# Half-array matmuls of a state mixing and of two attentions, reordered to alternate between the array's halves

## The chip, the cores and the metric

The kernel runs on one core of a Trainium2 chip, as one launch. The metric is the device time of a launch in microseconds; three runs of the kernel before took 2068.22, 2066.45 and 2060.09 us, median 2066.45. The core's engines work side by side, each through its own queue of instructions in order: PE (matmuls, with its weight loads shown apart as PEld), DVE (vector), ACT (activations), POOL (elementwise work off PSUM) and SP (which issues DMAs here). PE writes its results to PSUM, which has eight banks of 128 partitions by 512 fp32 values. PE's array has 128 rows (the contracted index, read from SBUF partitions) and 128 columns (the output's partitions). A matmul that needs only part of them names its corner with `tile_position=(row, column)`.

## The reference

Two layers over 512 latent tokens and 256 context tokens, 1024 features wide. Each layer: norm and modulation, an input projection, two mixers side by side, an output projection, and an MLP with squared ReLU. The parts that matter here:

- layer 0, attention: each of 8 query heads of 64 features (4 to each of 2 key heads) attends to all keys; latent queries see 6 tiles of 128 keys, context queries the 2 tiles of the context. Softmax, then the weighted sum of the values.
- layer 0, state mixing, in both directions over the tokens, per head with a 64x64 state S:

```
sa = S kk_t
S  = S * w_t - sa (kk_t * a_t) + v_t k_t
y_t = S r_t
```

- layer 1, attention: latent queries see the context, their own tile and its neighbours within 128 tokens, and a sink logit.
- layer 1, a second state model (chunks of 128 tokens), which the change touches by one buffer only.

## The kernel before, in words

Everything is written against a planner. The Python code emits instructions in an order that gives each a priority (`tc.high_priority()` raises it). The planner then fixes each engine's order before the run, from priorities and from when inputs are ready on its simulated timeline, and puts in the waits. Tiles with a tag share a number of buffers (`bufs`).

The first layer's mixers run in one phase (lines 846 to 1172). The state mixing goes by chunks of 32 tokens, 24 steps, each of which does one chunk of each direction `d`, with four pairs of heads `a`. The two heads `h` of a pair lie on the halves of the partitions, and the results of the two directions on the halves of the output's partitions. In `step` (lines 972 to 1021) a chunk goes: x from the state (line 987), `xs` on DVE, u (line 997, 32x32 corners), the two `vu` on DVE, the state's update s (line 1012), and the new state on DVE, which the next step's x needs. `prepare` (lines 908 to 970) makes, ahead of it, the products z (line 946) and xv (line 963). `outputs` (lines 1023 to 1042) makes y from the state (line 1032) and from `vu` (line 1033). x, xv and y are matmuls of 128 rows by 64 columns, with 64 moving columns, on column half `64 * d`. s uses 64 rows and 64 columns, in the corner (64 h, 64 h).

Before, x and xv ran through all four `a` of one direction and then of the other. y did so too, with the state's and the `vu` product of each `a` in turn. s ran through all directions and pairs of head 0 and then of head 1.

`attend` (lines 1088 to 1134) is the attention, a generator whose steps fill in between (`advance(fill)`); 40 of its steps come ahead of the state mixing. For each query tile and each half `g` of the heads it makes four heads' scores and their softmax into `prob` tiles. Then for each key tile four transposes go into a `pt` bank (line 1124), a copy of it goes to `pts` by DVE or ACT in turn (lines 1127 and 1129), and a value matmul goes into `po` (line 1130): 128 rows of keys, 64 columns, 512 moving columns. Half `g` of the heads took column half `g` of the array, accumulated over the key tiles, so that all matmuls of one `g` stood on one column half. `po` has one PSUM bank and `pt` two. A copy of `po` (line 1133) goes out by DMA at the end of the query tile.

`attend1` (lines 1476 to 1524) is the same for layer 1's four latent query tiles, with 4 or 5 key tiles each, one `pt` bank, and line 1518 for the value matmul. Its result is split at once into high and low parts in the place of the queries. `go` advances it at high priority, beside the input projection's column tiles, then beside the second state model (`own`, `rest`, `states`) and the first half of the output projection.

Of the kernel before, what the change touches and what calls it, by code (L numbers as in the profile page):

```python
# [18 lines left out]
P = 128  # L19
# [16 lines left out]
# the latents in the order in which the mixers finish them: the tiles in the middle, then the two outer ones  # L36
# [3 lines left out]
# order of the 128-token tiles and of the 64-token blocks for each direction  # L40
# [3 lines left out]
# column tiles of the second layer's input projection  # L44
F1_ORDER = ["B0", "B1", "C0", "C1", "x0", "x1", "x2", "x3", "k", "v", "q0", "q1", "q2", "q3"]
CONV_INDEX = {n: i for i, n in enumerate(["x0", "x1", "x2", "x3", "B0", "B1", "C0", "C1"])}
# column tiles of the first layer's input projection, in the order of their use
# [5 lines left out]
class Cols:  # L53
    """Named column ranges of a packed [128, n] array."""
# [15 lines left out]
def feat(a):  # L70
    """[..., n*128] -> [128, ... * n] with feature p of tile t in row p."""
    a = np.asarray(a)
    a = a.reshape(a.shape[:-1] + (a.shape[-1] // P, P))
    return np.moveaxis(a, -1, 0).reshape(P, -1)
# [41 lines left out]
def masks():  # L116
    """Constants of the second layer only."""
    f = np.float32
    c = Cols()
    m, n = np.arange(P)[:, None], np.arange(P)[None, :]  # L120
    c.add("upto", (m <= n).astype(f))
    c.add("from", (m >= n).astype(f))
    c.add("neg0", np.where(m > n, f(-1e30), f(0)))
    c.add("neg1", np.where(m < n, f(-1e30), f(0)))
    return c
# [38 lines left out]
# rows of the state mixing's output: tiles (a // 2, head of the pair), in them (a % 2, feature)  # L164
# [3 lines left out]
def tiles_k(w):  # L168
    """[K, n*128] -> [n, 128, K/128 * 128]: per column tile, the K tiles side by side."""
# [4 lines left out]
def pack(i):  # L174
# [8 lines left out]
    # the first layer's modulation weights: [group of 2048 columns, k tile, half, 128, 1024]  # L183
    o["wmod"] = np.ascontiguousarray(i["w_mod"].reshape(2, KT, P, 3, 2, 1024).transpose(0, 3, 1, 4, 2, 5)[0].reshape(3, KT, 2, P, 1024)[1:])
    # the second layer's: a column tile's columns in the rows, (row of the K tile, K tile) along them
    o["wmod1"] = np.ascontiguousarray(i["w_mod"][1].reshape(KT, P, 48, P).transpose(2, 3, 1, 0).reshape(48, P, D))
    # the first group's by quarters of the features: [quarter, pair of k tiles, 128, (k tile, shift or scale, 256)]
# [11 lines left out]
    # z: tokens by features, per half of the features two pieces of four K tiles  # L199
# [5 lines left out]
    # [layer, group, pair of column tiles, 128, (column tile, k tile, 128)]  # L205
# [5 lines left out]
class Stream:  # L211
    """The residual of both streams, tile by tile."""
# [12 lines left out]
def tile_trunk(ctx: ExitStack, tc: tile.TileContext, t: dict, out, cc: Cols, pc: Cols):  # L225
# [20 lines left out]
    # the unit matrix and the ones first  # L246
# [14 lines left out]
    def psum_pool(stack, side="left", **tags):  # L261
        """PSUM of a phase: per tag, its number of tiles and of banks per tile, or the tag that it shares."""
# [3 lines left out]
    def psum(tag, name):  # L266
# [3 lines left out]
        if isinstance(v, list):  # L270
            # in turn
# [5 lines left out]
    def split(hi, lo, src, lo_eng=None):  # L277
        """hi + lo = src exactly, each in the 12 bits that one pass carries."""
# [12 lines left out]
    def cols2(seg):  # L291
        """Columns of a two-bank PSUM tile that hold a segment's tokens."""
        return slice(256 + seg[0], 256 + seg[0] + seg[1])

    def at(t, s):
        """A segment's columns of t, [128, tokens]."""
# [4 lines left out]
    def like(t, s):  # L301
        """Side by side columns in the shape of a segment's."""
        return t.rearrange("p (b c) -> p b c", c=P) if s == OUTER else t

    class Split:
        """A PSUM tile [128, tokens] whose streams lie in a bank each."""
# [7 lines left out]
    class One(Split):  # L314
        """A PSUM tile that holds a segment."""
# [4 lines left out]
        def __call__(self, s):  # L320
            return self.ps[:, 0:s[1]]

# [9 lines left out]
    def product(items, xh, xl, ks, segs, first=True, last=True, k0=0):  # L332
        """ps[128, tokens] (+)= W^T x for the K tiles ks and each of the items (ps, W, first column in W), K tile by K tile.

        W and x as hi and lo parts; W's K tiles count from k0 on."""
# [10 lines left out]
    # ---------------------------------------------------------------- modulation  # L346
    def sigmoid(out, in_, tmp, halfbias=None):
        """1 / (1 + exp(-x)) = (tanh(x / 2) + 1) / 2."""
# [6 lines left out]
    def rsqrt(out, in_, scale, eps, n):  # L355
        """(in_ * scale + eps) ** -0.5 of n columns."""
# [15 lines left out]
    def modulation(l, j):  # L372
        """Shift, scale and gate columns 2048 j.. of layer l, one K tile per step."""
# [21 lines left out]
    def first_modulation(q, np_):  # L395
        """Shift and scale of the first layer's projections, for a quarter of the features."""
# [27 lines left out]
    def norm_scale(l, which, wname, a=None, k=0, n=KT):  # L424
        """norm weight * (1 + scale), per feature and stream."""
# [10 lines left out]
    # ---------------------------------------------------------------- norms  # L436
# [3 lines left out]
    def add_squares(np_, acc, x, k, s, eng=G):  # L440
        """Adds the squares of feature tile k to the sums of a stream's tokens."""
# [7 lines left out]
    def rms_rows(np_, acc, s, tag):  # L449
        """1 / rms of each of a stream's tokens, broadcast over the partitions."""  # L450
# [18 lines left out]
    def norm_tile(np_, x, bc, a, l, shift, hh, hl, s, k, eng):  # L469
        """hi and lo parts of x / rms * a + shift, feature tile k."""  # L470
# [10 lines left out]
    def norm_mod(np_, x, acc, a, l, shift, hh, hl, s, tag):  # L481
        """hi and lo parts of x / rms * a + shift."""
# [5 lines left out]
    # ---------------------------------------------------------------- layer 0: projections and what needs no state  # L488
# [16 lines left out]
    with ExitStack() as sa:  # L505
# [4 lines left out]
        # 1 - mu_prev - mu_next  # L510
# [3 lines left out]
        with ExitStack() as sx:  # L514
# [13 lines left out]
            # the first column tiles go along with the quarters of the features  # L528
# [23 lines left out]
        # sums start again with every chunk  # L552
# [18 lines left out]
        def shifted(n, name, bufs=2, ps=None, copy=False):  # L571
            """Column tile n, mixed with the tokens before and after within its stream."""
# [15 lines left out]
        def tile_of(ps, i):  # L588
            """Columns of the i-th 128 tokens."""
# [3 lines left out]
        def token_sums(ps, c, sq):  # L593
            """Per token and half of the partitions, the sum of sq: columns c.. of ps."""
# [3 lines left out]
        def token_broadcast(r, name):  # L598
            """[tokens, (tile, half)] -> a row per token, over the partitions of each half."""
# [32 lines left out]
        def load_k(p):  # L632
            """Keys of a pair of heads, and their unit vectors."""
# [17 lines left out]
        def load_v(p):  # L651
            v = vs[p] = shifted(5 + 3 * p, "fv", 2)
            # tokens of v to the partitions
# [1138 lines left out]
```

## Time and profile before

| | |
|---|---|
| median of 3 runs | 2066.45 us |
| lowest, highest | 2060.09, 2068.22 us |
| span of the profiled execution | 2059.2 us |
| its mean granted TensorE clock | 0.977 |
| state mixing and attention, first x to last po | 397.7 to 703.3 us |
| layer 1's value matmuls, first to last | 1448.0 to 1658.3 us |

The profile is of one execution, and its span runs from the first to the last instruction; the launch's own time was not recorded apart from the three runs, which lie 0.9 to 9.0 us above that span. In the rows, "L987" is line 987 of the kernel, `x<-state,ard` names the tile written and those read, and `128*64 128x64` is rows by columns of the array and the moving operand. Each fp32 matmul leaves two records, each with its weight load. A matmul's duration includes its latency through the array, so that neighbours overlap in the records.

### The profile page before, as it was taken

To read this page: it belongs to the slowest core of one execution; us is meant where nothing else is said; L and a number is where in the kernel's file an instruction comes from. 1 tells how busy PE (TensorE), PEld (TensorE's weight loads), DVE (VectorE), ACT (ScalarE), POOL (GpSimd) and SP (SyncE) were. 2 spreads that over 40 slices of the span, in tenths; PEclk is the share of its full clock that TensorE was granted. 3 is DMA by queue.
4 is the path that set the end of the run, shared out by engine and by line. 5 is a ranking of instruction groups with operands and counts; after the bars stand their busy time and mean duration, and the time that the engine had idled before them with its cause. 6 is when DMAs were issued, how large, how long until landed. Compare 5 with 4: busy or idle time off the path is not lost.

```text
span 2059.2 us, 34221 instructions
## 1 busy us (share of the span) xinstructions
PE 1945.9 (94%) x13992; PEld 1593.0 (77%) x13992; DVE 1211.2 (59%) x2057; ACT 826.5 (40%) x1397; POOL 374.2 (18%) x379
## 2 busy tenths in 40 slices
PE   6999978799999989999999999999979999999997
PEld 4776656587777689888888888888856888888886
DVE  6466889556456666565455443677577574444445
ACT  4333333344444354222222332545466654333335
POOL 0033268322122152000000000321033120000002
PEclk9999998699999999999999999999999999999998
DMA  8445455742231473333444442311100133333333
GB/s 318 136 146 195 164 189 149 156 91 49 65 76 35 130 237 110 103 123 119 134 127 124 128 128 72 104 56 56 58 21 1 52 123 91 94 92 102 93 94 112
DMA packets 148173, 229.24 MB, mean 111 GB/s; under 512 B 65056, under 2 KB 102320, under 8 KB 147888
## 3 DMA queue, kind: packets, MB, share of 16 engines
q1 hardware_dynamic: 141200, 214.59, 34.7%
q10 hardware_dynamic: 5456, 7.73, 1.2%
q0 software_dynamic: 1360, 4.73, 0.7%
q8 instruction: 110, 1.80, 0.4%
q14 instruction: 47, 0.39, 0.1%
HBM read 200.53 MB, written 26.48 MB: 110 GB/s over the span
## 4 chain that ended last, share of the span: by engine, by line
PE 74%; DVE 11%; DMA 6%; POOL 3%; issue 3%; ACT 3%; SPq 0%; DVEq 0%; POOLq 0%; ACTq 0%
PE m L343 36%; PE win L343 10%; DMA wmod<-in_wmod_dram 4%; PE po L1130 2%; PE z L946 2%; PE s L1012 2%; DVE wlo L280 2%; PE po L1518 2%; PE pt L1124 2%; PE sc L1109 1%; PE y L1033 1%; PE wout L1276 1%; DVE junk L1293 1%; PE z L1548 1%; PE y L1032 1%
## 5 line engine op out<-in xcount | busy, mean ns | idle before, releaser
L279 ACT ACTIVATE whi<-wraw 128x1024 fp32r<-128x1024 f32 x214 | 226.4, 1059 | 663.8 <-PE m L343 561.5
L280 DVE TENSOR_TENSOR wlo<-wraw,whi 128x1024 fp32r<-128x1024 f32 x214 | 264.8, 1239 | 196.3 <-ACT whi L279 193.7
L343 PE MATMUL m<-hh,whi 128*128 128x512 f32 (+1 forms) x816 | 240.4, 344 | 3.8 <-ACT relu L1215 2.2
L343 PE MATMUL m<-hh,wlo 128*128 128x512 f32 (+1 forms) x816 | 241.5, 344 | 0.4 <-DVE wlo L280 0.4
L343 PE MATMUL m<-hl,whi 128*128 128x512 f32 (+1 forms) x816 | 241.5, 343 | 0.2 <-POOL hl L479 0.2
L343 PE MATMUL m<-dl,whi 128*128 128x256 f32 (+1 forms) x832 | 240.7, 341 | 0.0
L343 PE MATMUL m<-dh,whi 128*128 128x256 f32 (+1 forms) x832 | 238.6, 342 | 2.1 <-DVE xl L1197 1.9
L343 PE MATMUL m<-dh,wlo 128*128 128x256 f32 (+1 forms) x832 | 239.8, 341 | 0.1
L447 POOL TENSOR_TENSOR acc<-acc,nsq 128x256 f32<-128x256 f32 x42 | 43.2, 1036 | 854.0 <-ACT nsq L446 853.3
L343 PEld LDWEIGHTS m<-dh,whi 128*128 128x128 f32 x832 | 153.3, 188 | 24.2 <-DVE xl L1197 5.3
L343 PEld LDWEIGHTS m<-hh,whi 128*128 128x128 f32 x816 | 152.6, 188 | 23.7 <-ACT relu L1215 2.6
L343 PEld LDWEIGHTS m<-hh,wlo 128*128 128x128 f32 x816 | 153.4, 188 | 19.8 <-DVE wlo L280 1.1
L343 PEld LDWEIGHTS m<-hl,whi 128*128 128x128 f32 x816 | 153.6, 188 | 19.3 <-POOL hl L479 0.4
L343 PEld LDWEIGHTS m<-dl,whi 128*128 128x128 f32 x832 | 153.8, 188 | 19.0
L343 PEld LDWEIGHTS m<-dh,wlo 128*128 128x128 f32 x832 | 153.6, 188 | 18.9 <-DVE wlo L280 0.3
L343 PE MATMUL win<-hl,whi 128*128 128x512 f32 (+1 forms) x512 | 161.7, 349 | 4.9 <-POOL hl L479 3.5
L343 PE MATMUL win<-hh,whi 128*128 128x512 f32 (+1 forms) x512 | 158.2, 355 | 1.7 <-ACT hh L474 1.6
L343 PE MATMUL win<-hh,wlo 128*128 128x512 f32 (+1 forms) x512 | 159.0, 344 | 0.0
L1293 DVE SCALAR_TENSOR_TENSOR junk<-wmod,crow 128x1024 f32<-128x1024 f32 x64 | 78.4, 1225 | 115.4 <-DMA wmod<-in_wmod_dram 114.9
L1197 DVE SCALAR_TENSOR_TENSOR xl<-m,modT,xl 128x512 f32<-128x512 f32 (+1 forms) x144 | 97.3, 685 | 72.3 <-PE m L343 72.3
L343 PEld LDWEIGHTS win<-hh,whi 128*128 128x128 f32 x512 | 95.5, 193 | 29.1 <-issue 7.2
L343 PEld LDWEIGHTS win<-hl,whi 128*128 128x128 f32 x512 | 98.2, 193 | 20.8 <-POOL hl L479 4.7
(411 smaller groups left out, 3717.0 us busy)
## 6 DMA issues: line engine op xcount, KB each, us to landing
wraw<-in_w_dram SPq DMA_DIRECT2D x136, 512.0 KB, 3.5
wmod<-in_wmod_dram SPq DMA_DIRECT2D x96, 512.0 KB, 4.2
wraw<-in_wout_dram SPq DMA_DIRECT2D x40, 512.0 KB, 3.6
wraw<-in_win_dram SPq DMA_DIRECT2D x35, 512.0 KB, 3.9
arD<-ar SPq DMA_DIRECT2D x8, 768.0 KB, 3.8
kbD<-kb SPq DMA_DIRECT2D x8, 768.0 KB, 4.4
ari<-arD SPq DMA_DIRECT2D x24, 256.0 KB, 3.8
kbd<-kbD SPq DMA_DIRECT2D x48, 128.0 KB, 3.7
```

Source lines behind the costliest of these rows:

```text
L279: A.activation(out=hi, in_=src, func=AF.Copy)
L280: (lo_eng or V).tensor_tensor(out=lo, in0=src, in1=hi.bitcast(F32), op=ALU.subtract)
L343: T.matmul(part(ps, s), lhsT=a[:, c], rhs=row(b, k, s), start=first and j == 0 and q == 0, stop=last and j == n - 1 and q == 2)
L447: (V if k == KT - 1 else eng).tensor_tensor(out=at(acc, s), in0=at(acc, s), in1=at(sq, s), op=ALU.add)
L946: T.matmul(ps[:, P * (2 * a + c):P * (2 * a + c) + P], lhsT=kb[:, 2 * m + a, c, :], rhs=ar[:, 2 * m + a, c, :], start=True, stop=True)
L1012: T.matmul(pd[r, 256 * d + 64 * a:256 * d + 64 * a + 64], lhsT=zs[d][r, a, cl[d], 64:128], rhs=vu[d][r, a, :], start=True, stop=True, tile ...
L1032: T.matmul(o, lhsT=ars[d][:, a, c, 0, :], rhs=state[:, d, a, :], start=True, stop=False, tile_position=(0, 64 * d))
L1124: T.transpose(pt[:, P * j:P * j + P], prob[j][:, P * (kt - kt0):P * (kt - kt0) + P], ident)
L1130: T.matmul(po[r, :], lhsT=vtok[:, kt, r], rhs=pts, start=kt == kt0, stop=kt == kt1 - 1, tile_position=(0, 64 * g))
L1197: V.scalar_tensor_tensor(out=xs, in0=part(ps, s), scalar=mod(l, which, m, s[2]), in1=xs, op0=ALU.mult, op1=ALU.add)
L1293: V.scalar_tensor_tensor(out=junk, in0=wm, scalar=1.0, in1=crow[:, :, v], op0=ALU.mult, op1=ALU.mult, accum_out=modT[:, l, n, v:v + 1])
L1518: T.matmul(po[r, :], lhsT=vt1[:, kt, r], rhs=pts, start=m == 0, stop=m == len(kts) - 1, tile_position=(0, 64 * g))
```

## The change

It computes the same and changes the order in which half-array matmuls are issued.

- xv, x and y: the loop over `a` is outside and that over the directions inside, so that consecutive matmuls alternate between column halves. In y the state's products of both directions come, then the `vu` products of both.
- s: head `h` is the innermost loop, so that consecutive matmuls alternate between opposite corners.
- both attentions use a new function `weighted`. Even key tiles take column half 0 and odd ones column half 1, for the same half of the heads, and the two value matmuls of a pair of key tiles are issued together. The two sums over even and odd tiles are added at the end of each half of the heads: an ACT copy of one and a DVE addition of the other. `po` is taken once per half of the heads, not once per query tile.
- buffers: `pts` 3 for 2; in layer 1 the result `o` takes a buffer of the `prob` tag, `st` has 5 for 6 and `xd` 2 for 3.

```diff
+    def weighted(prob, vt, g, kts, o, pool):
+        r, po, n = HALVES[g], psum("po", "po"), len(kts)
+        pair = []
+        for m, kt in enumerate(kts):
+            pt = psum("pt", "pt")
+            for j in range(4):
+                T.transpose(pt[:, P * j:P * j + P], prob[j][:, P * m:P * m + P], ident)
+            w = pool.tile([P, 512], F32, tag="pts", name=u("pts"), bufs=3)
+            if m % 2 == 1:
+                V.tensor_copy(out=w, in_=pt)
+            else:
+                A.activation(out=w, in_=pt, func=AF.Copy)
+            pair.append((m, kt, w))
+            if len(pair) == 2 or m == n - 1:
+                for i, (m_, k_, w_) in enumerate(pair):
+                    T.matmul(po[HALVES[i], :], lhsT=vt[:, k_, r], rhs=w_, start=m_ < 2, stop=m_ + 2 >= n, tile_position=(0, 64 * i))
+                pair = []
+            yield
+        A.activation(out=o[r], in_=po[HALVES[1], :], func=AF.Copy)
+        V.tensor_tensor(out=o[r], in0=po[HALVES[0], :], in1=o[r], op=ALU.add)
...
                     px = psum("zy", "xv")
-                    for d in (0, 1):
-                        c = 1 - j if d else j
-                        for a in range(4):
+                    for a in range(4):
+                        for d in (0, 1):
+                            c = 1 - j if d else j
...
                 px = psum("ch", "x")
-                for d in (0, 1):
-                    for a in range(4):
+                for a in range(4):
+                    for d in (0, 1):
...
             pd = psum("ch", "s")
-            for h in (0, 1):
-                for d in (0, 1):
-                    for a in range(4):
+            for d in (0, 1):
+                for a in range(4):
+                    for h in (0, 1):
...
             py = psum("zy", "y")
-            for d in (0, 1):
-                c = 1 - j if d else j
-                for a in range(4):
-                    o = py[64 * d:64 * d + 64, 64 * a:64 * a + 64]
-                    if state is not None:
-                        T.matmul(o, lhsT=ars[d][:, a, c, 0, :], rhs=state[:, d, a, :], start=True, stop=False, tile_position=(0, 64 * d))
-                    T.matmul(o, lhsT=zs[d][:, a, c, 0:64], rhs=vu[d][:, a, :], start=state is None, stop=True, tile_position=(0, 64 * d))
+            for a in range(4):
+                o = [py[64 * d:64 * d + 64, 64 * a:64 * a + 64] for d in (0, 1)]
+                if state is not None:
+                    for d, c in enumerate((j, 1 - j)):
+                        T.matmul(o[d], lhsT=ars[d][:, a, c, 0, :], rhs=state[:, d, a, :], start=True, stop=False, tile_position=(0, 64 * d))
+                for d, c in enumerate((j, 1 - j)):
+                    T.matmul(o[d], lhsT=zs[d][:, a, c, 0:64], rhs=vu[d][:, a, :], start=state is None, stop=True, tile_position=(0, 64 * d))
...
-            po = psum("po", "po")
...
+            o = tp.tile([P, 512], F32, tag="oa", name=u("oa"), bufs=1)
...
-                    T.matmul(po[r, :], lhsT=vtok[:, kt, r], rhs=pts, start=kt == kt0, stop=kt == kt1 - 1, tile_position=(0, 64 * g))
-                    yield
-            o = tp.tile([P, 4, P], F32, tag="oa", name=u("oa"), bufs=1)
-            A.activation(out=o.rearrange("p a c -> p (a c)"), in_=po, func=AF.Copy)
-            nc.scalar.dma_start(oD[0:4, :, P * qi:P * qi + P].rearrange("a q c -> q a c"), o)
+                yield from weighted(prob, vtok, g, list(range(kt0, kt1)), o, tp)
+            nc.scalar.dma_start(oD[0:4, :, P * qi:P * qi + P].rearrange("a q c -> q a c"), o.rearrange("p (a c) -> p a c", c=P))
...
-            po = psum("po", "po")
+            o = tp.tile([P, 640], F32, tag="prob", name=u("oa"), bufs=6)[:, 0:512]
...
-                    st = tp.tile([P, 6], F32, tag="st", name=u("st"), bufs=6)
+                    st = tp.tile([P, 6], F32, tag="st", name=u("st"), bufs=5)
...
-                    T.matmul(po[r, :], lhsT=vt1[:, kt, r], rhs=pts, start=m == 0, stop=m == len(kts) - 1, tile_position=(0, 64 * g))
-                    yield
...
-            oh, ol = (q1[:, m, :, P * (qi - 2):P * (qi - 2) + P] for m in (0, 1))
-            pv = po.rearrange("p (a c) -> p a c", c=P)
-            A.activation(out=oh, in_=pv, func=AF.Copy)
-            V.tensor_tensor(out=ol, in0=pv, in1=oh.bitcast(F32), op=ALU.subtract)
+                yield from weighted(prob, vt1, g, kts, o, tp)
+
+            split(*(q1[:, m, :, P * (qi - 2):P * (qi - 2) + P] for m in (0, 1)), o.rearrange("p (a c) -> p a c", c=P))
...
-                x_ = sp.tile([P, 8, 64], F32, tag="xd", name=u("xd"), bufs=3)
+                x_ = sp.tile([P, 8, 64], F32, tag="xd", name=u("xd"), bufs=2)
```

More of the change, by code (lines that the diff above doesn't have):

```diff
@@ L1099, in attend @@
             V.tensor_tensor(out=qs[64:128], in0=qr[64:128], in1=qs[64:128].bitcast(F32), op=ALU.subtract)
+            o = tp.tile([P, 512], F32, tag="oa", name=u("oa"), bufs=1)
             for g in (0, 1):
-                r = HALVES[g]
                 prob = []
@@ L1120, in attend @@
                     yield
-                for kt in range(kt0, kt1):
-                    pt = psum("pt", "pt")
-                    for j in range(4):
-                        T.transpose(pt[:, P * j:P * j + P], prob[j][:, P * (kt - kt0):P * (kt - kt0) + P], ident)
-                    pts = tp.tile([P, 512], F32, tag="pts", name=u("pts"), bufs=2)
-                    if kt % 2 == 1:
-                        V.tensor_copy(out=pts, in_=pt)
-                    else:
-                        A.activation(out=pts, in_=pt, func=AF.Copy)
-                    T.matmul(po[r, :], lhsT=vtok[:, kt, r], rhs=pts, start=kt == kt0, stop=kt == kt1 - 1, tile_position=(0, 64 * g))
-                    yield
-            o = tp.tile([P, 4, P], F32, tag="oa", name=u("oa"), bufs=1)
-            A.activation(out=o.rearrange("p a c -> p (a c)"), in_=po, func=AF.Copy)
-            nc.scalar.dma_start(oD[0:4, :, P * qi:P * qi + P].rearrange("a q c -> q a c"), o)
+                yield from weighted(prob, vtok, g, list(range(kt0, kt1)), o, tp)
+            nc.scalar.dma_start(oD[0:4, :, P * qi:P * qi + P].rearrange("a q c -> q a c"), o.rearrange("p (a c) -> p a c", c=P))
         def state_mixing(fill):
@@ L1480, in attend1 @@
             kts = [0, 1] + list(range(lo, hi))
-            po = psum("po", "po")
+            o = tp.tile([P, 640], F32, tag="prob", name=u("oa"), bufs=6)[:, 0:512]
             for g in (0, 1):
-                r = slice(64 * g, 64 * g + 64)
                 prob = []
@@ L1508, in attend1 @@
                     yield
-                for m, kt in enumerate(kts):
-                    pt = psum("pt", "pt")
-                    for j in range(4):
-                        T.transpose(pt[:, P * j:P * j + P], prob[j][:, P * m:P * m + P], ident)
-                    pts = tp.tile([P, 512], F32, tag="pts", name=u("pts"), bufs=2)
-                    if m % 2 == 1:
-                        V.tensor_copy(out=pts, in_=pt)
-                    else:
-                        A.activation(out=pts, in_=pt, func=AF.Copy)
-                    T.matmul(po[r, :], lhsT=vt1[:, kt, r], rhs=pts, start=m == 0, stop=m == len(kts) - 1, tile_position=(0, 64 * g))
-                    yield
-            oh, ol = (q1[:, m, :, P * (qi - 2):P * (qi - 2) + P] for m in (0, 1))
-            pv = po.rearrange("p (a c) -> p a c", c=P)
-            A.activation(out=oh, in_=pv, func=AF.Copy)
-            V.tensor_tensor(out=ol, in0=pv, in1=oh.bitcast(F32), op=ALU.subtract)
+                yield from weighted(prob, vt1, g, kts, o, tp)
+            split(*(q1[:, m, :, P * (qi - 2):P * (qi - 2) + P] for m in (0, 1)), o.rearrange("p (a c) -> p a c", c=P))
         attention = steps(*(attend1(qi) for qi in range(2, NTT)))
```

## The prediction

> **What bounds the kernel now.** I read the page first, then the stage that the change touches most, by windows, by waits and by the chain that ended last.
>
> ```profile
> span 2059.2 us, 34221 instructions
> PE 1945.9 (94%) x13992; PEld 1593.0 (77%) x13992; DVE 1211.2 (59%) x2057; ACT 826.5 (40%) x1397; POOL 374.2 (18%) x379
> ```
> ```profile
> core 0: us, PE busy (x) PEld busy (x) DVE busy (x) ACT busy (x) POOL busy (x), PEclk, DMA share, GB/s
> 400.00:700.00 300.00, 297.51 (x3698) 223.13 (x3696) 171.39 (x396) 134.86 (x258) 72.98 (x66) 1.00 0.27 65
> ```
> ```profile
> PE u L997 <- DVE xs L990: 0.5, 1, 0.5
> PE z L946 <- ACT xv L966: 0.5, 1, 0.5
> ```
>
> The first layer's state mixing with the attention beside it fills the window from 400 to 700 us. PE is busy for 297.5 of 300 us at full clock, and its longest waits in that window are the two of 0.5 us. DVE has 171 us of work there and ACT 135. So the stage is as long as PE's queue. PE's busy time counts the latency of each matmul, so a duration is not what one costs; the cost is the distance to the next start. The change touches these lines, counted in records, of which each fp32 matmul leaves two:
>
> ```profile
> L963 PE MATMUL xv<-vm,zk x384: 221/222/369, 366.5 to 683.9; 128*64 128x64 f32 x192
> L987 PE MATMUL x<-state,ard x368: 221/222/369, 397.7 to 690.6; 128*64 128x64 f32 x184
> L1012 PE MATMUL s<-vu,z x736: 217/218/366, 390.3 to 688.8; 64*64 64x64 f32 x184
> L1032 PE MATMUL y<-state,ard x368: 222/222/271, 402.8 to 696.2; 128*64 128x64 f32 x184
> L1033 PE MATMUL y<-vu,z x384: 219/222/369, 387.3 to 696.3; 128*64 128x64 f32 x192
> L1130 PE MATMUL po<-pts,vtok x112: 592/592/692, 398.6 to 703.3; 128*64 128x512 f32 x112
> L1518 PE MATMUL po<-pts,vt x72: 592/643/1116, 1448.0 to 1658.3; 128*64 128x512 f32 x72
> ```
>
> The chain gives their distances, since its pieces on PE run from start to next start (the two rows of po are the first and the last of ten such pieces of four records):
>
> ```profile
> 420.97 1.86 PE po L1130 x4
> 440.60 0.12 PE y L1032 x2
> 442.39 0.90 PE x L987 x16
> 447.90 1.83 PE s L1012 x32
> 473.69 0.57 PE xv L963 x13
> 670.17 1.86 PE po L1130 x4
> ```
>
> A record of 64 columns thus takes 56 to 58 ns of PE (0.90/16, 1.83/32, 0.12/2), and one of po 465 (1.86/4). The 44 ns of xv are a first sign that some of it overlaps already.
>
> **Do two halves run at once?** The change only reorders; it pays if a matmul on one half of the array runs beside one on the other. The trace of before has cases of it:
>
> ```profile
> 504.62 0.22 PE L1032 MATMUL y<-state,ard 128*64 128x64 f32 x1
> 504.62 0.27 PE L963 MATMUL xv<-vm,zk 128*64 128x64 f32 x1
> 504.68 0.22 PE L1032 MATMUL y<-state,ard 128*64 128x64 f32 x1
> 504.73 0.22 PE L963 MATMUL xv<-vm,zk 128*64 128x64 f32 x1
> 504.74 0.22 PE L1033 MATMUL y<-vu,z 128*64 128x64 f32 x1
> 504.79 0.22 PE L963 MATMUL xv<-vm,zk 128*64 128x64 f32 x1
> 504.79 0.22 PE L1033 MATMUL y<-vu,z 128*64 128x64 f32 x1
> ```
> ```profile
> 67.41 1.68 PE L381 MATMUL mod<-wmod,cs 128*32 128x512 f32 x8
> 202.46 1.71 PE L762 MATMUL ab<-kb,ar 64*32 64x32 f32 x96
> 444.61 0.61 PE u L997 x32
> ```
>
> Where the end of y (second direction) meets the start of xv (first direction), starts come in twos: from 504.73 on each line goes every 0.06 us and both go together, 29 ns per record. The modulation's 512-column matmuls alternate between two column tiles: eight records in 1.68 us with the last one's latency, where four of po take 1.86. The triangles alternate row halves and take 18 ns per record (1.71/96); the 32x32 tiles of u take 19 (0.61/32). So both kinds of halves overlap, and PE can issue faster than the 29 ns per record needed here.
>
> **Part by part.** A group that alternates should last half its records times 58 ns.
> - State update s (L1012): 23 groups, 1.83 to 16 x 0.058 = 0.93 us, 0.90 less each: 20.7 us.
> - x (L987): 23 groups, 0.90 to 8 x 0.058 = 0.46: 10.1 us.
> - xv (L963): 24 groups of 16 records, between 0.70 (16 x 44 ns) and 0.90 now; 0.46 after: 5.8 to 10.6, I take 7.
> - Outputs y (L1032, L1033): 752 records x 58 ns = 43.6 us; half is 21.8. Some stand beside xv already, and those of one direction may be ready before the other's: I take 19, between 10 and 22.
> - Attention values po (L1130): 56 matmuls become 28 pairs; a pair that stands together should take half of 1.86 us, 0.93 less. How many do is the open term. PE's queue is filled by readiness, so the second of a pair may find other work put ahead of it:
>
> ```profile
> 517.41 1.07 PE L1130 MATMUL po<-pts,vtok 128*64 128x512 f32 x2
> 518.42 0.44 PE L1124 MATMUL pt<-cst,prob 128*128 128x128 f32 x2
> 518.78 0.64 PE L1130 MATMUL po<-pts,vtok 128*64 128x512 f32 x1
> ```
>
> Here a transpose stands between two of them. The ten pieces of four records above are neighbours already. Ends: 10 pairs (9.3 us) and 28 (26 us); I take 16, nearer to the ten that the trace shows: 15 us.
>
> The sum in this stage is 20.7 + 10.1 + 7 + 19 + 15 = 72 us of PE's queue, with ends of 56 and 89.
>
> **What the shorter queue uncovers.** Each of the 23 steps has three waits on DVE, now covered by other PE work: u for xs, s for both vu, the next x for the state.
>
> ```profile
> L1002 DVE SCALAR_TENSOR_TENSOR vu<-u,cst,vm 128x256 f32<-128x256 f32 x46 | 20.0, 476 | 6.5 <-PE u L997 6.4
> L1020 DVE TENSOR_TENSOR state<-s,old 128x512 f32<-128x512 f32 x22 | 15.2, 691 | 37.6 <-PE s L1012 35.6 <-POOL ard L937 2.0
> L990 DVE TENSOR_TENSOR xs<-x,xv 128x256 f32<-128x256 f32 x22 | 9.3, 421 | 4.1 <-ACT xv L966 2.4 <-PE x L987 1.0
> L1133 ACT ACTIVATE oa<-po 128x512 f32<-128x512 f32 x5 | 3.0, 597 | 11.9 <-PE po L1130 11.9
> ```
>
> That is 0.42 + 2 x 0.48 + 0.69 = 2.1 us per step, 48 us in all if nothing covered them. The matmuls z, the scores and the transposes keep their length and still stand there, but y, xv and po, the other covers, are halved. I take a quarter lost, 12 us; bounds 0 and 48. That leaves 60.
>
> The added work lies off PE: each half of the heads gets an ACT copy and a DVE addition of 64x512 where one copy of 0.60 us stood per query tile. For 12 halves, by the rows of 0.60 and 0.69 us above, that is at most 7.2 - 3.6 = 3.6 us on ACT and 8.3 on DVE; with them they have 139 and 180 us for a stage of some 240. The addition also holds po's one bank: the next half's first value matmul waits for it, but four heads of scores lie between. The third buffer of pts removes a wait that the page hardly shows. I cost these at nothing; without cover they are 12 x 1.3 = 16 us, a bound that I keep in the range.
>
> **The second layer.** 36 value matmuls become 16 pairs and 4 single ones, each 1.00 us now, so 14 us at most (16 x 0.86, two records of 0.43). But transposes have one bank there:
>
> ```profile
> 1631.58 0.44 PE pt L1512 x4
> 1632.02 1.00 PE po L1518 x2
> 1633.02 2.35 PE wout L1706 x18
> ```
>
> The next transposes go, then one value matmul, then other products while the copy that the other half of a pair needs is made. I take three pairs together, 2.6 us. Against it: o takes one of the six prob buffers, so one head fewer is prepared ahead; xd and st lose a buffer each; and the last tile's end grows by a copy and an addition, 1.3 us. Net 1 us gained; bounds -8 (the eight halves' 1.3 us each, less the pairs) and +14.
>
> **Sum.** 2059.2 - 60 - 1 = 1998 us of span. The three times lie 0.9 to 9.0 us above that span (2060.09 to 2068.22); with 5 for what lies around, I forecast **2003 us**, 3.1% under the median of 2066.45.
>
> **Two rules against it.** The Trainium skill says, in "TensorE: Matmul & The Clock Gate", Part 3, The mechanism, that weight loads overlap running matmuls only when their row groups differ. In x, xv, y and po both halves use all 128 rows, so by that rule only s would gain; the seven rows at 504.62 speak against it, as both lines there have all rows. In "TensorEngine Tiling (Array Packing)", PSUM Pressure, it says that different row tiles cannot use one PSUM bank at the same time. By that s would keep its 1.83 us and the forecast would be some 20 us higher; the triangles' 18 ns per record, with row halves writing the same bank, speak against it.
>
> **The rivals.** Times are spans plus 5.
> - *The waits take over.* DVE's answers are uncovered for three quarters or all of their length: 72 - 36 to 72 - 48, so 24 to 36 us less in this stage, and 1 in the other: 2027 to 2039. For it: all engines' orders are fixed before the run, and less PE work stands in each gap. Against: x at 442.39 takes 0.90 us and xs 0.42, so u could have started near 443.8 and did at 444.61; with u's 0.61 and both vu s could have started near 446.4 and did at 447.90. Both were late by order, not by need. 16%, with all from 2018 up.
> - *Everything pairs.* All 28 and 16 pairs stand together, y gains fully and nothing is uncovered: 89 + 14 = 103 us less, 1961. Half of what separates it from the forecast gives 1982. 10%, for 1961 to 1988. Against: the transpose at 518.42.
> - *Column halves share what loads weights*, and only s gains: 20.7 us, 2043. 3%: the rows at 504.62 would have to be an exception.
> - *Row halves can't write one bank together*, and s alone keeps its time: 60 - 20.7 + 1 us less, 2024. 2%, inside the first rival's range.
> - *The order is undone.* PE's queue is filled by readiness, and the directions' inputs (two vu, two sets of keys) come at different times, so that only x, whose inputs are all there, alternates: 10.1 us less a quarter for the waits, 2057, within 0.5%. Against: the same 1.5 us by which s came late. 4%.
> - *Slower: switching halves costs and nothing overlaps.* In the rows above the first xv after the switch took 0.27 us, its followers 0.22: 48 ns in between. The change adds 6 switches to each group of x and xv and 14 to each of s and y: 6 x 47 + 14 x 47 = 940, at 48 ns 45 us: 2109. It decides once a switch costs more than the overlap saves, 58 ns for every record that runs beside another. Against: u switches tile with every matmul at 19 ns. 4%.
>
> **How the numbers follow.** The forecast's own case, 1988 to 2018, has 61%. The range leaves out column halves, the undone order, the slower case and the better half of the second rival, 16% in all: 1978 to 2040. Faster by over 0.5% (10 us, about what a measurement of this kernel tells from no change): 0.61 + 0.16 + 0.10 + 0.03 + 0.02 = 0.92; within it 0.04; slower 0.04.
>
> **What would show it.** Right: the chain's pieces of s near 0.93 us for 32 records and of x near 0.46 for 16; y and xv starting in twos; po in fours over 0.93; the stage from the first x (397.7) to the last po (703.3) some 60 us shorter; new PE waits for xs, vu and the state of about 12 us. Wrong: s and x at their old distances (the halves don't overlap), PE waits of 30 us and more (the waits take over), transposes or z between the two of most pairs, or a second layer longer than its 1448 to 1658 us.

## The result, and the profile after

| | before | changed |
|---|---|---|
| median of four runs each | 2067.07 us | 2032.47 us |
| lowest to highest | 2060.09 to 2068.22 | 2029.92 to 2040.03 |
| span of the profiled execution | 2059.2 | 2030.2 |

The ratio is 0.9857, with an interval of 0.9825 to 0.9889: 23 to 36 us less. The forecast was 2003 us and 63 us less. The sign was right and so was the mechanism of the gain, but the forecast gain was about twice what came, and the second layer moved the other way.

First the page of the changed kernel (span; then busy time, share and instructions of each engine), and a table by windows of the stage's body and of its end, whose columns are those of the prediction's second fence:

```profile
span 2030.2 us, 34262 instructions
PE 1890.3 (93%) x13992; PEld 1546.9 (76%) x13992; DVE 1222.5 (60%) x2077; ACT 833.7 (41%) x1411; POOL 380.7 (19%) x379
```
```profile
400.00:640.00 240.00, 231.81 (x3460) 169.59 (x3458) 165.89 (x378) 134.28 (x255) 69.95 (x63) 1.00 0.32 73
640.00:660.00 20.00, 6.36 (x148) 5.25 (x148) 11.27 (x25) 2.19 (x3) 5.41 (x4) 0.74 0.68 209
```

PE did the same 13992 matmul records in 56 us less of busy time, so most of the intended saving is there. In the first layer's stage PE is still nearly full to 640 us (231.8 of 240 us). Then it stands almost empty for 20 us, 6.4 us busy, where the same place of the kernel before, its last 20 us around the end of po, was filled:

```profile
690.00:710.00 20.00, 18.39 (x160) 11.86 (x160) 15.31 (x30) 7.76 (x11) 2.57 (x4) 1.00 0.81 261
```

The waits of PE in that stage after the change (total, times, longest) put more than half of it in one row, the output projection that waits for the attention's and the mixing's result:

```profile
PE wout L1287 <- ACT xr L279: 12.1, 1, 12.1
PE y L1057 <- DVE vu L1026: 3.2, 5, 1.3
PE xv L987 <- DVE zk L976: 1.0, 2, 0.6
PE sc L1132 <- ACT prob L1139: 1.0, 4, 0.3
PE y L1055 <- ACT z L979: 1.0, 2, 0.6
```

To find where time was won and given back I cut both spans at the same three places: the first y, the first wout and layer 1's first rot. Their first starts are in the rows by line (first and last start in us); the kernel before, whose first y (387.3) stands in the prediction:

```profile
L1276 PE MATMUL wout<-xr,whi x128: 276/279/388, 703.8 to 732.1; 128*128 128x256 f32 x128
L1387 PE MATMUL rot<-rraw,cst x10: 591/592/697, 1362.7 to 1403.5; 128*128 128x512 f32 x10
```
and the changed one:
```profile
L1057 PE MATMUL y<-vu,z x384: 219/222/369, 385.1 to 647.8; 128*64 128x64 f32 x192
L1287 PE MATMUL wout<-xr,whi x128: 276/279/579, 660.2 to 690.7; 128*128 128x256 f32 x128
L1398 PE MATMUL rot<-rraw,cst x10: 591/592/697, 1312.5 to 1353.0; 128*128 128x512 f32 x10
```

| stretch, us | before | changed | difference |
|---|---|---|---|
| start to first y | 387.3 | 385.1 | -2.2 |
| first y to first wout (mixing and attention of layer 0) | 316.5 | 275.1 | -41.4 |
| first wout to first rot of layer 1 | 658.9 | 652.3 | -6.6 |
| first rot to the end (layer 1's attention, second state model, projection, MLP) | 696.5 | 717.7 | +21.2 |
| span | 2059.2 | 2030.2 | -29.0 |

The spans are of one execution each, and differ by 29.0 us where the medians differ by 34.6.

So two questions are open. Why did the first stage give 41 us, 48 with what the projection gained behind it (most of the 6.6 is its own length, 85.1 to 79.3 us), and not 60? And why did the second layer, forecast 1 us shorter, become 21 us longer?

**The second layer.** There the first sign is in ACT's timeline (start, duration, engine, line, operation, and in brackets the idle time ahead with its releaser). Each `prob<-sc` of L1504 is the first copy of one head's scores. In the changed kernel the fourth and the fifth of them are 49 us apart, though PE had the fifth head's scores done at 1368.05:

```profile
1363.08 0.60 ACT L1504 ACTIVATE prob<-sc 128x512 f32<-128x512 f32 x1
...
1411.71 0.59 ACT L344 ACTIVATE oa<-po 64x512 f32<-64x512 f32 x1 [1.39 <-PE po L341]
1412.33 0.60 ACT L1504 ACTIVATE prob<-sc 128x512 f32<-128x512 f32 x1
```

The fifth head begins only behind the first write of `oa`, the result that now takes a buffer of the prob tag. In the kernel before, six heads were copied (1395.9 to 1423.6) ahead of the first value matmul at 1448, the fifth and the sixth of them here:

```profile
1419.32 0.59 ACT L1494 ACTIVATE prob<-sc 128x512 f32<-128x512 f32 x1
1423.56 0.60 ACT L1494 ACTIVATE prob<-sc 128x512 f32<-128x512 f32 x1 [0.23 <-PE sc L1491]
```

Later in the layer PE waits for prob, and the granted clock falls. The waits from 1500 to 1642 us, and a window of 80 us that begins 250 us after the first rot:

```profile
PE pt L332 <- ACT prob L1516: 6.6, 5, 2.1
PE sc L1500 <- ACT prob L1504: 3.9, 4, 1.3
```
```profile
1562.00:1642.00 80.00, 65.61 (x370) 45.78 (x370) 38.93 (x79) 41.27 (x91) 14.23 (x17) 0.85 0.17 52
```
The same window of the kernel before:
```profile
1613.00:1693.00 80.00, 77.97 (x576) 68.59 (x576) 55.80 (x107) 45.49 (x93) 19.67 (x21) 1.00 0.35 111
```

PE was busy 66 of 80 us at a clock of 0.85, where it had been busy 78 at full clock. Over the whole stretch from the first rot to the end, 13.7 of the 21.2 us are PE standing idle (44.5 us against 30.8), and 7.5 are its 3590 records, as many as before, taking 673.3 us for 665.7, at a mean granted clock of 0.97 for 0.98.

### The profile page after: what moved, and what is told of

It is laid out like the page before. It is cut to its first block, busy times and chain, and to the rows that moved or that the text cites. A ratio compares the mean times of both kernels' runs of the same rounds, so it can differ in the third digit from the quotient of the medians.

```text
span 2030.2 us, 34262 instructions
## 1 busy us (share of the span) xinstructions
PE 1890.3 (93%) x13992; PEld 1546.9 (76%) x13992; DVE 1222.5 (60%) x2077; ACT 833.7 (41%) x1411; POOL 380.7 (19%) x379
## 4 chain that ended last, share of the span: by engine, by line
PE 72%; DVE 11%; DMA 7%; POOL 3%; ACT 3%; issue 3%; SPq 0%; DVEq 0%; POOLq 0%; ACTq 0%
PE m L367 37%; PE win L367 11%; DMA wmod<-in_wmod_dram 5%; PE po L341 4%; PE pt L332 2%; PE z L970 2%; PE wout L1287 2%; DVE wlo L280 2%; PE wout L1703 1%; PE sc L1132 1%; PE s L1036 1%; DVE junk L1304 1%; PE z L1545 1%; PE mod L405 1%; PE y L1057 1%
```

## Experiments

All ratios are to the kernel before, run on the same chip. Stretches are cut as in the table above: "stage" is first y to first wout, "layer 1" is first rot to the end. These stretches are of one execution of each kernel, and their spread is several us: the time to the first y runs from 381.6 to 387.9 us over kernels whose difference from one another lies behind it.

### Which part gave, which took: the attention of layer 1 undone; only the mixing

`l1_old` is the changed kernel with `attend1` and its buffers (prob 6, st 6, xd 3) as before; `mix_only` also has `attend` of layer 0 as before, so that x, xv, s and y alone alternate.

```diff
-                yield from weighted(prob, vt1, g, kts, o, tp)
+                for m, kt in enumerate(kts):
...
+                    T.matmul(po[r, :], lhsT=vt1[:, kt, r], rhs=pts, start=m == 0, stop=m == len(kts) - 1, tile_position=(0, 64 * g))
```

> The changed kernel with the second layer's attention of before (its value matmuls, its buffers: six prob tiles for heads only, st 6, xd 3). Theory: the second layer's attention cost the changed kernel some 20 us (its head start over the kernel before shrinks from 50 us at the second layer's first products to 30 us at its last value matmul), so about 2012 us. Rival: the layer lost its time to another order of the planner's that the first layer brings with it: about 2032 us.

> Only the state mixing alternates (x, xv, s, y); both attentions are those of before. Theory: the trace of the changed kernel shows PE's time for s 17.7, x 8.5, y 11.5 and xv 1.4 us shorter, 39 in all; all attention work stays as filler, so the end is covered as before and 30 to 39 us show: 2028 to 2037 us. Rival: the halved value matmuls carried most of the gain: 2045 us or more.

| | ratio | median | stage | layer 1 |
|---|---|---|---|---|
| l1_old | 0.9784 [0.9757, 0.9812] | 2013.26 | 274.4 | 701.3 |
| mix_only | 0.9824 [0.9805, 0.9843] | 2022.44 | 276.5 | 701.8 |
| l1_old, again | 0.9786 [0.9765, 0.9806] | 2016.43 | 275.5 | 700.1 |

Undoing one function of the change makes it 15 us faster (0.9784 against 0.9857): the second layer's pairing costs that much as it was made. The mixing alone is worth 36 us, 40 of them in the stage (276.5 against 316.5). The pairs of layer 0 add some 8 us to it by the whole times (the two intervals touch), but only 2 in the stage, though PE's time for po falls by 15. With them PE is busy in the stage for 252.9 us, where `mix_only` has 267.5, and it stands idle for 21.5, where `mix_only` has 9.0: most of what the pairs free is spent in waits, 3.7 us of it in the wait before the first wout and the rest inside the stage. The rest of the 8 us lies ahead of the first y and between wout and rot, and no run shows that it belongs to the pairs.

### What in layer 1 costs: the buffer or the pairing

`o_own` gives the result a buffer of its own and leaves prob five; `old_prob5` has the old attention with five prob buffers and five of `st`; `o6p2` keeps the pairing, gives the result its own buffer beside six prob buffers, and takes the room from pts (2 for 3).

```diff
-            o = tp.tile([P, 640], F32, tag="prob", name=u("oa"), bufs=6)[:, 0:512]
+            o = tp.tile([P, 512], F32, tag="oa", name=u("oa"), bufs=1)
...
-            w = pool.tile([P, 512], F32, tag="pts", name=u("pts"), bufs=3)
+            w = pool.tile([P, 512], F32, tag="pts", name=u("pts"), bufs=2)
```

> The changed kernel with the second layer's o in a buffer of its own and five prob tiles, which is the same memory for the same number of heads ahead. Theory (the claim): o stands in the ring of prob tiles, so the next heads' first copies wait until o's first write, behind the values; with a buffer of its own five heads go ahead of the first values and 10 to 20 us come back: 2012 to 2022 us. Rival (the buffers): one head fewer ahead, or the addition and copy at each half's end, cost the time: no change, 2030 us or more.

> The changed kernel with the second layer's attention of before, once more, as the measure of the next three. All theories: the same ratio as in its first run, 0.978 (2013 us there).

> The changed kernel with the second layer's attention of before, but with five prob buffers and five st buffers there, and no result among them: one head fewer can be prepared ahead, and nothing else of the pairing is there. Theory: the head that isn't prepared ahead is itself the main cost of the pairing in the second layer, 6 to 12 us of the 15, so this is 6 to 12 us longer than with six buffers. Rival: the second layer loses by the pairing itself (a value matmul that waits for the second key tile's copy, the copy and the addition at the end of each half of the heads), and five buffers alone cost under 3 us.

> The changed kernel with the second layer's pairing kept, but the result in a buffer of its own beside six prob buffers, and two buffers for pts in place of three, to make the room. Theory (buffers): the whole ring of six is back, so most of the 15 us that the second layer gave back returns: within 4 us of the kernel with the second layer's attention of before. Rival (the pairing itself): it stays 8 us or more longer than that one, as with the result in a buffer of its own and five prob buffers. A loss beyond that is the missing third pts buffer, as the first copy of the next pair then waits for the pair before.

| | ratio | median | layer 1 | heads copied ahead |
|---|---|---|---|---|
| changed kernel: result in the ring of six | 0.9857 [0.9825, 0.9889] | 2032.47 | 717.7 | 4 |
| o_own: own buffer, ring of five | 0.9829 [0.9804, 0.9853] | 2021.56 | 706.6 | 5 |
| old_prob5: old attention, ring of five | 0.9843 [0.9819, 0.9867] | 2026.12 | 713.3 | 5 |
| l1_old, again: old attention, ring of six | 0.9786 [0.9765, 0.9806] | 2016.43 | 700.1 | 6 |
| o6p2: own buffer, ring of six | 0.9756 [0.9734, 0.9779] | 2010.83 | 695.2 | 6 |

The theory of the buffers holds. One prob buffer less costs 11 to 13 us of layer 1 whether the values are paired (o_own against o6p2) or not (old_prob5 against l1_old), and the whole times agree, 15 and 12 us with intervals apart. `o_own` itself came out at the edge of its expectation: 11 us of layer 1 return, but by the ratios the whole gains only 6, with intervals that overlap. The rival, that the pairing itself costs, falls: with the ring whole again, the paired layer is about as short as before the change (695.2 against 696.5). ACT's timeline of `o6p2` shows the fifth and sixth heads where they were missing:

```profile
1362.38 0.60 ACT L1504 ACTIVATE prob<-sc 128x512 f32<-128x512 f32 x1
...
1368.17 0.59 ACT L1504 ACTIVATE prob<-sc 128x512 f32<-128x512 f32 x1
...
1372.41 0.60 ACT L1504 ACTIVATE prob<-sc 128x512 f32<-128x512 f32 x1 [0.23 <-PE sc L1501]
```
Its longest PE waits from 1500 to 1642 us no longer name prob, and the window that begins 250 us after its first rot is full:
```profile
PE wout L1703 <- ACT q L279: 2.1, 1, 2.1
PE m L367 <- ACT whi L279: 1.2, 1, 1.2
```
```profile
1562.00:1642.00 80.00, 76.48 (x571) 67.72 (x570) 56.62 (x106) 44.95 (x90) 19.61 (x19) 1.00 0.37 113
```

`o6p2` also has the lowest ratio of the study, though its interval overlaps with that of `l1_old`. That its layer 1 is 1.3 us shorter than before, near the 1 us of the forecast, is luck. `o6p2_raw` (below), whose layer 1 has the same code, takes 699.7 us there, 3.2 longer than before; against the unpaired `raw_act`, run beside it, its layer 1 is 0.7 us shorter, where `o6p2` against `l1_old, again` has 4.9. And the pairs are not in the trace: in `o6p2` no two value matmuls of layer 1 run side by side (two that stand together take 1.86 us, where a pair of layer 0 takes 1.01), and PE's time for all of them is 39.4 us against 39.6 before. So a gain from the pairing in layer 1 is not shown; what is shown is that, once the ring is whole, it costs nothing that these runs can tell.

### What y is worth

`y_old` is `l1_old` with the products of y in their old order, one direction after the other.

```diff
-            for a in range(4):
-                o = [py[64 * d:64 * d + 64, 64 * a:64 * a + 64] for d in (0, 1)]
...
+            for d in (0, 1):
+                c = 1 - j if d else j
+                for a in range(4):
```

> The changed kernel with the second layer's attention of before, and with y in its old order (one direction's eight products, then the other's). Theory: the alternation of y is worth what the trace shows of it, 11.5 us in the state mixing, so this is about 11 us longer than the same kernel with y alternating. Rival: it is worth the 19 us of the prediction, and the planner's tearing of y takes nothing: 19 us longer. Second rival: the torn fragments pay as much for entering and leaving the half-array order as they gain, and the gain seen in y is that of its neighbours: within 4 us.

Measured: 2034.35 us, ratio 0.9874 [0.9854, 0.9894], 18 us longer than `l1_old` in the same batch. By the time alone the rival with 19 us would have won. The stretches say otherwise: of the 20.6 us by which the two spans differ, 8.4 lie in the stage, 4.5 ahead of the first y, 2.7 between wout and rot, and 5.0 in layer 1, whose code is the same in both. In the stage PE's time for y is 51.9 us against 38.7, that is 13 more; 6.4 of it is hidden, as the wait before the first wout falls from 12.4 to 6.0 us. So the term of y is 8 to 13 us. The 12 us in other stretches can't be put down to it: the 4.5 ahead of the first y lie within the spread of that stretch, and both there and in layer 1 the granted clock of this execution was lower (0.91 for 0.94, 0.97 for 0.98). No run here shows whether the order of y has a part in that; the order of instructions is planned anew with each change.

### The pairs of layer 0 alone

`att0_only` is the kernel before with `attend` of the change, and nothing else of it.

> The kernel before with the first layer's attention alone in pairs; mixing and second layer as before. Theory: the pairs save the 15 us of TensorE time that the changed kernel's trace shows in po, but the attention is what filled TensorE to the stage's end at 703.9 us, 7.3 us past the last y, so the state mixing's end sets the stage and a part goes into the seam: 7 to 11 us shorter than before. Rival 1: all of it counts, 14 us or more. Rival 2: the switches between full and half array eat it, and the gain of 8 us seen between two of the earlier kernels is the planner's: within 3 us of before.

Measured: 2052.86 us, ratio 0.997 [0.9953, 0.9986], 6 us less, between 3 and 10. PE's time for po falls from 51.1 to 42.5 us, since only 9 pairs stand together here, and then a wait that was not there before takes most of it:

```profile
PE wout L1287 <- ACT xr L279: 6.7, 1, 6.7
```

The stage is 2.3 us shorter (314.2), as between `mix_only` and `l1_old`: PE is busy in it for 302.8 us where it was 313.7, and idle for 11.4 where it was 2.9. The theory's mechanism is right, its size too high. The first rival falls. The second is right in size for the stage, but not in its cause, since po's time does fall and waits take it.

### The wait at the seam

The projection's first load, `raw<-oD`, stands on SP behind four loads of gates. In `l1_old, again`:

```profile
644.33 0.38 SPq L1072 DMA_DIRECT2D gg<-g1D  x1
644.77 0.50 SPq L1073 DMA_DIRECT2D gg<-g2D  x1
646.51 0.36 SPq L1072 DMA_DIRECT2D gg<-g1D  x1
646.92 0.56 SPq L1073 DMA_DIRECT2D gg<-g2D  x1
647.67 7.38 SPq L1278 DMA_DIRECT2D raw<-oD  x4
```

It looks as if the queue's order made PE wait. `raw_pool` (on the changed kernel) and `raw_act` (on `l1_old`) put the context's load on POOL's and on ACT's queue; `o6p2_raw` does the latter on `o6p2`.

```diff
-                    nc.sync.dma_start(o[:, :, P * (b or 0):P * (b or 0) + n], oD[4 * half:4 * half + 4, :, c:c + n].rearrange("k p n -> p k n"))
+                    (nc.scalar if s == CTX_SEG else nc.sync).dma_start(o[:, :, P * (b or 0):P * (b or 0) + n], oD[4 * half:4 * half + 4, :, c:c + n].rearrange("k p n -> p k n"))
```

> The changed kernel with the context's load of both mixers' outputs (raw from oD) issued on POOL's queue, where it stands on SP's behind the gates' loads. Theory (the seam): the load starts 4 us or more earlier and PE's wait of 12.1 us ahead of the first output projection shrinks to 4 to 8 us: 2024 to 2028 us. Rival: the memory that the load goes to is free only with the end of the state mixing, so the load starts no earlier: 2032 us.

> The changed kernel with the second layer's attention of before, and the first load of the output projection (raw, the context) issued on ACT's queue, where it stands behind the last xv copies and ahead of ACT's 12.5 us wait for the last group norm, and not on SP behind four loads of gates. Theory: at the seam TensorE waits for a load that is issued too late on its queue, so the wait of 12 us before the first wout falls to 3 to 6 us and the kernel is 6 to 9 us shorter than with the load on SP, about 2007 us. Rival: the load's buffer comes free only with the end of the state mixing, so it is issued no earlier than at 648 us on ACT too: no change within 2 us, and the wait stays at 12 us.

> The whole change, with the second layer's result in a buffer of its own beside six prob buffers and two pts buffers, and the context's load on ACT's queue: both repairs together. Theory: they add, as one lies in the first layer's end and the other in the second layer: 0.9756 less 3 to 4 per mille, a ratio of 0.971 to 0.973, near 2003 us, the time that was predicted for the change alone. Rival: if the load gains nothing, 0.9756.

Measured: `raw_pool` 2038.87, ratio 0.9906 [0.9883, 0.993], 0.5% behind the changed kernel with intervals that touch: its load was issued at 651 us, behind POOL's own stores, and PE's wait grew from 12.1 to 17.5 us; `raw_act` 2015.03, 0.9778 [0.9765, 0.9791], no change; `o6p2_raw` 2015.59, 0.9783 [0.9769, 0.9797], 0.27% behind `o6p2`. So none of the three gained what its theory said. The rows by line of the load in `raw_act` (shortest/median/longest in ns, first and last start) say why:

```profile
L1278 ACTq EVENT_SEMAPHORE  x4: 38/38/7784, 641.3 to 649.7; - x4
L1278 ACTq DMA_DIRECT2D raw<-oD x2: 367/408/450, 649.3 to 649.8; - x2
```

```profile
648.33 0.87 DVE L1026 SCALAR_TENSOR_TENSOR vu<-u,cst,vm 128x256 f32<-128x256 f32 x2
```

ACT's queue came to the load at 641.3 us and stood 7.8 us on semaphores. It issued at 649.27, right behind the last vu of the mixing, which DVE's timeline (last fence) shows to end at 649.20. So on ACT's queue the load is held by the chain's last step. On SP it came 2.6 us behind that step (in `l1_old, again` the last vu ends at 645.09), and that much the queue's order can have cost. Its buffer is in a pool that is opened when the mixing's memory is given back, which would explain the hold; that the memory is the reason was not tried. PE's wait before the first wout did fall, from 12.4 to 6.9 us, which the rival did not expect, and the stage became 6 us shorter (269.3). But the projection behind it waited again for the second half of the load, and wout to rot grew by 4.4 us. So the rival holds in the main: the seam is the state chain's own end plus the load's 4 to 12 us to landing, and neither of the two other queues removes it.

## Why the prediction missed

Three steps failed, by size: "Net 1 us gained" for the second layer, where the lost prob buffer had no price and 21 us were lost; the stage set equal to PE's queue up to its end, where a wait of 12 us came that the sum had no term for; and "a group that alternates should last half its records times 58 ns", by which the five terms were put too high.

**What held.** PE's queue is still most of the bound (PE is busy for 253.0 of the stage's 275.1 us), and halves run at once. The chain of waits of the changed kernel, whose pieces run to the next start, shows it (start, length, line, records):

```profile
407.24 1.08 PE s L1036 x32
410.98 0.61 PE x L1011 x16
420.51 1.01 PE po L341 x4
568.22 0.64 PE xv L987 x16
569.38 0.69 PE xv L987 x14
```

s went from 1.83 to 1.08 us, x from 0.90 to 0.61, four records of po from 1.86 to 1.01. No whole group of x or s kept its old length (the first of s, at a granted clock of 0.50 in both, went from 3.24 to 1.90 us), so the rivals of column halves that share the weight loading, of row halves that cannot share a bank, and of switches that cost more than they save all fall. The two rules of the Trainium skill that were weighed against the change ("TensorE: Matmul & The Clock Gate", Part 3, The mechanism; "TensorEngine Tiling (Array Packing)", PSUM Pressure) do not describe these traces: x and s both issue a record every 29 ns inside a group. The order was not undone either: 17 of the 28 pairs of po stand together, where 16 were taken. PE's idle time inside the stage, without the wait before wout, is 10.0 us where it was 2.8, so 7 us are new, where 12 were taken; most of it is for vu, z and zk, 0.7 for xs, and none for the state.

**The terms of the stage.** PE's time, summed over the distances from each record of the stage to the next start:

| term | before | changed | measured | forecast |
|---|---|---|---|---|
| s | 43.4 | 25.7 | -17.7 | -20.7 |
| x | 20.9 | 12.4 | -8.5 | -10.1 |
| xv | 18.6 | 17.2 | -1.4 | -7 |
| y | 49.9 | 38.4 | -11.5 | -19 |
| po | 51.1 | 36.3 | -14.8 | -15 |
| all else (z, scores, transposes, u) | 132.5 | 132.9 | +0.4 | 0 |
| the wait before wout | 0 | 12.1 | +12.1 | 0 |

The five terms give 54 us with the new waits inside them, where the forecast had 72 less 12. They were mis-sized by one step of the prediction: "a group that alternates should last half its records times 58 ns". A group has ends that do not halve. Of the 0.61 us of x, 8 x 58 ns are 0.46 and 0.15 us more go at its two ends; s (0.93 + 0.15) shows the same. In the kernel before these ends were invisible, because the groups already overlapped by about three records where the direction changes (16 x 58 ns + 0.15 - 3 x 58 ns = 0.90), so that 0.90/16 looked like a plain distance. For xv, with 44 ns, that overlap was a larger share and is what the prediction called a first sign; halving left it 0.64 to 0.69 per group. The prediction also put y at 43.6 us before, by 58 ns a record, where 49.9 are measured. And y does not stand as one group: it comes in 106 pieces of 1 to 28 records, seven in the mean, between scores, values and transposes. The timeline of one such piece, whose starts do come in twos:

```profile
483.08 0.27 PE L1057 MATMUL y<-vu,z 128*64 128x64 f32 x1
483.09 0.27 PE L1055 MATMUL y<-state,ard 128*64 128x64 f32 x1
483.19 0.22 PE L1057 MATMUL y<-vu,z 128*64 128x64 f32 x1
483.20 0.27 PE L1055 MATMUL y<-state,ard 128*64 128x64 f32 x2
483.25 0.22 PE L1057 MATMUL y<-vu,z 128*64 128x64 f32 x1
483.31 0.22 PE L1055 MATMUL y<-state,ard 128*64 128x64 f32 x1
483.31 0.22 PE L1057 MATMUL y<-vu,z 128*64 128x64 f32 x1
483.46 0.39 PE L1132 MATMUL sc<-kh,qs 128*128 128x256 f32 x1
```

Eight records take 0.38 us (483.08 to 483.46), 0.23 of work and 0.15 of ends. Four such pieces a step are 1.5 us, where half of 32 x 58 ns is 0.93. In `mix_only`, with the old attention between, y costs 34.6 us and xv 14.4. The difference to the table is mostly waits: in the changed kernel 4.5 us of y's time and 2.1 of xv's are PE waiting, in `mix_only` 0.2 and 0.5. So with the pairs of po the state's chain is no longer fully covered, which is why po's 15 us of PE time shorten the stage by only 2.

**The seam.** The prediction set the stage equal to PE's queue and let the whole saving count. Each saving in the filler also brings nearer the point where it runs out: po ended 7 us after the last y in the kernel before and ends 11 us ahead of it now (637 against 648 us). From there the recurrent chain stands bare, and behind it the load. That is the 12 us of the first row of waits, less what the projection gained behind it. "The waits take over" was looked for inside the steps; it came mostly once, at the end, and the prediction had no term for it. The measured 2032 us lie in that rival's 2027 to 2039, but by chance: it wanted 24 us and more uncovered in the steps and nothing lost in the second layer.

**The second layer.** This was the largest error, 21 us lost where 1 gained was forecast and -8 was the bound. The prediction named the cause, "o takes one of the six prob buffers, so one head fewer is prepared ahead", and gave it no price: the 1.3 us that it sets against the pairs are a copy and an addition. It costs two heads, not one (4 ahead, not 6), and about 11 us for each (717.7 against 706.6, 706.6 against 695.2), 7 for the second by `o6p2_raw`. The prediction's own sign of being wrong came with it: the layer's value matmuls, first to last, take 230.5 us (1397.1 to 1627.6) where they took 210.3. Of the three pairs that it took to stand together there, one does in the changed kernel and none in `o6p2`. Why the claim costs two heads when it takes one of six buffers, no run here shows.

Put together, for the spans: 53.9 from the five terms, less 0.4 for the rest of the stage and 12.1 for the seam, 6.6 back behind it, 21.2 lost in layer 1 and 2.2 won ahead of the first y make 29.0 us, where 61 were forecast. How much of the 21.2 is the lower clock alone, and how much the gaps that came with it, no run here separates.

## What to carry to other kernels

Interleaving matmuls that use different parts of the array pays in the length of the uninterrupted group: about 0.15 us per group did not shrink here, so look at how many pieces the planner makes of it. A shorter filler must be followed to its end: ask what the filler covered last, and what that waits for; here the pairs of the first attention saved PE 15 us and shortened the stage by 2. Before a buffer is taken from a ring, count how many steps the ring lets the producer run ahead; one buffer of six was worth 7 to 13 us of the second layer.

## What was not expected of the hardware

Two halves of the array overlap a little even without interleaving. In a group of x of the kernel before, records come every 58 ns in two series. The second direction's, told apart by this spacing alone, starts at 442.607 us, while the first direction's still come at 442.601, 442.659 and 442.717, about three records ahead of its turn. A change from a group on half arrays to one on full arrays and back costs about 0.15 us, for x with 16 records as for s with 32 and for pieces of y with 4 and 8 (0.27 and 0.38 us); pieces with other neighbours show 0.05 to 0.2. The granted clock was low where PE had gaps: 0.74 in the 20 us of the seam, 0.85 in the stretch of layer 1 where it waited for prob, 1.00 in that stretch when the ring was whole.
